# Hybrid diffusion step on one core: weights times values two key tiles at a time, the maxima's row in F32R, neighbourhood tiles of six whole key blocks

## The chip, the cores and the metric

The kernel runs on one core of a Trainium2 chip. A time is the device time of one execution in microseconds (us). TensorE (PE, with its weight loads as PEld), VectorE (DVE), ScalarE (ACT), GpSimd (POOL) and SyncE (SP, which issues DMA) each work through a queue of their own, in order; semaphores join them.

## The reference

Two layers of a transformer trunk work on 1024 latent tokens and 128 prompt tokens of width 1024. A layer has modulated RMS norms, one input projection, three parallel head groups (a convolution module, grouped-query attention with 6 query and 2 key heads of 64, and neighbourhood attention with 6 heads), an output projection, and a squared-ReLU MLP. The two attentions of the latent tokens are what matters here:

```python
# grouped-query: 1024 latent keys and 128 cached context keys
p = softmax(einsum('bqhgd,bkhd->bhgqk', q, k) * Dh ** -0.5)
o = einsum('bhgqk,bkhd->bqhgd', p, v)
# neighbourhood: a latent row of the 16 x 64 grid sees 8 grid rows x 16 columns, and the context
s_loc = where(col_mask, einsum(qr, kr) * scale + bias, NEG_INF)
s_ctx = einsum(qr, kc) * scale
p = softmax(concatenate([s_loc, s_ctx], axis=-1))
o = einsum(p_loc, vr) + einsum(p_ctx, vc)
```

The prompt tokens attend to the prompt alone.

## The kernel before

Everything is F32. Scores and projections split an operand into an F32R part and its rest, and run as F32R products; weights times values, transposes and the row of the maxima are plain F32, which PE does in two passes per product (the page counts both). The order of each engine's instructions is the order in which the program writes them; generators (`prep`, `prompt`, `end`, `natten`, `conv_out`) are advanced by hand so that their pieces lie between those of the main loop. Every PSUM tile is one of eight banks (`P`); SBUF tiles come from the pools S (18), T (18), U (19) and V (24), reused as earlier tiles are read out.

**Grouped-query attention** (`gqa`, L1001) has six units a layer: three pairs of heads, each with two halves of 512 queries. A unit goes over nine key tiles of 128 (eight latent, one of context). A step `kt` makes, for both heads, scores with keys in the partitions (psst, L1132 and L1133; the 65th row of q2 carries the negative maximum of each query), their exponentials on ACT into `pt`, one `side()`, then `late()` of the step before, then another `side()`. `late` is `pv`: weights times values into the accumulator psacc (L1118: two heads in the two halves of PE's columns, so four instructions a key tile), and the sum of `pt` into R (L1120; POOL up to kt 6, DVE after).

`side()` advances the preparation of the next unit (`prep`, L1013): transposes of its queries; twelve calls that each issue two products psm (128 queries by 384 keys, L1044) and their maxima on DVE (mx, L1046); `down` (L1027), which reduces the three maxima of each query to nmx (L1029); `spread` (L1032), which turns nmx into a row by four products with the identity (psnm, L1035), copied by ACT into partition 64 of q2 (L1036). `down(0)` and `spread(0)` come inside the scan, `down(1)` and `spread(1)` behind it, at kt 7. `side()` also advances the prompt's attention and the end of the unit before (pssum, rr, rt). The rest of the convolution (cacc, lsq, lrs, lsg) is spread over the same time on DVE and ACT.

**Neighbourhood attention** (`natten`, L1152) goes over tiles of 128 queries (two grid rows) for two heads at a time. In step `i` it makes the scores of tile i (`scores_na`, L892), its exponentials, the end of tile i-3, transposes of tile i-1 (pspt, L969) with their copies out of PSUM (L977), and weights times values of tile i-2 (pspv, L985), with pieces of the next pair's preparation between. Edge tiles (t below 2 or above 5) see 8 grid rows and the context, 640 keys. Inner tiles see 9 rows and the context, 704 keys: four blocks of 128, the context's 128, and a last block of 64:

```python
self.blocks = [(128 * i, 128, v(r0 // 2 + i)) for i in range(4)]
self.blocks += [(512, 128, vc)] if edge else [(576, 128, vc), (512, 64, v(t + 2, 64))]
```

POOL adds the column mask to the biases of the next pair (L1166 to L1168, `end_bias`), spreads the reciprocal sums (r, L955), and makes the low part of the result (L99, HA<-cc).

Of the kernel before, what the change touches and what calls it, by code (L numbers as in the profile page):

```python
# [45 lines left out]
def hybrid_step(ctx, tc, I, O, depth=DEPTH):  # L46
# [1 line left out]
    pers = ctx.enter_context(tc.tile_pool(name="pers", bufs=1))  # L48
    dram = ctx.enter_context(tc.tile_pool(name="dram", bufs=1, space=bass.MemoryType.DRAM))
    psum = ctx.enter_context(tc.tile_pool(name="psum", bufs=1, space=bass.MemoryType.PSUM))  # L50
    N_S, N_T, N_U = 18, 18, 19

    count = [0]
    def nm(p):
# [9 lines left out]
    def U(shape, dt=F32, n="u"):  # L64
        return pers.tile([128] + list(shape), dt, tag="U", bufs=N_U, name=nm(n))

    def V(shape, n="v"):
        return pers.tile([128] + list(shape), F32, tag="V", bufs=24, name=nm(n))

    def h_views():  # L70

# [34 lines left out]
        nc.vector.tensor_scalar(out=out, in0=a, scalar1=s1, scalar2=s2, op0=op0, **k)  # L106

    ident = pers.tile([128, 128], F32, name="ident")
    ones = pers.tile([128, 128], F32, name="ones")
    eps = pers.tile([128, 1], F32, name="eps")  # L110
    colmask = pers.tile([128, 64], F32, name="colmask")
# [231 lines left out]
    def prologue(pr):  # L343
        nc.scalar.preload_act_table_set("natural_log_exp_and_others")
        make_identity(nc, ident)
        nc.vector.memset(ones, 1.0)
        nc.vector.memset(eps, EPS)
        cc = U([KT, 2], n="cc")
        xt = [S([1024], n="xt") for _ in range(4)]
        for i in range(4):  # L350
            load(xt[i], I["x_sample"][i * 128:(i + 1) * 128, :])
        load(cc, I["cc"])
        load(vecs[0], I["vecs"][0])
        xh = [HF[8 + i][:, 0:1024] for i in range(4)]
        for i in range(4):
            load(xh[i], I["x_sample"][(i + 4) * 128:(i + 5) * 128, :])
        xp = [T([512], n="xtp") for _ in range(2)]
        for b in range(2):
            load(xp[b], I["x_prompt"][:, b * 512:(b + 1) * 512])
        m0 = modulation(0, [0], True)  # L360
        next(m0)
        sg = U([KT, 2], n="sg")
        sigmoid_of(sg, cc)
        tt(silc, cc, sg, ALU.mult)
        norms = [Norm(si) for si in range(3)]
        for k in range(KT):
            X[k] = S([2, HT], n="X")
        run(x_in(0, lambda i, k: xt[i][:, k * 128:(k + 1) * 128], norms[0]))
        del xt
        run(x_in(1, lambda i, k: xh[i][:, k * 128:(k + 1) * 128], norms[1]))  # L370
        next(m0)
        pr.fetch()
        pr.fetch()
        run(x_in(2, lambda i, k: xp[k // 4][:, k % 4 * 128:(k % 4 + 1) * 128], norms[2]))
        del xp
        for _ in range(4):
            next(m0)
        gs = [nrm.rstd() for nrm in norms]
        for _ in range(2):
            for g in gs:  # L380
                next(g)
        run(gs[0])
        for _ in range(2):
            next(m0)
        pr.prep(nc.gpsimd)
        for _ in range(2):
            pr.fetch()
        load(colmask, I["colmask"])
        for l in range(1, depth):
            load(vecs[l], I["vecs"][l])  # L390
        spill(0, 0)
        spill(0, 1)
        run(m0)
        first = norm1(pr.L, 0, norms[0], True)
        next(first)
        pr.prep()
        run(first)
        for g in gs[1:]:
            run(g)
        pr.prep()  # L400
        yield
        yield from together(norm1(pr.L, 2, norms[2], True), norm1(pr.L, 1, norms[1], True))
# [466 lines left out]
    class Direct:  # L869
# [9 lines left out]
        def scores_prompt(self, qs):  # L879
            ps = P("pssp")  # L880
            self.p, self.nmx = [], []
            for j in range(2):
                self.score(ps[:, j * 128:(j + 1) * 128], qs[j], self.kb[j].kp)
            for j in range(2):
                mx = V([1], "mx")
                nc.vector.tensor_reduce(out=mx, in_=ps[:, j * 128:(j + 1) * 128], op=ALU.max, axis=AX.X, negate=True)
                self.p.append(U([128], n="pp"))
                self.nmx.append(mx)
            self.blocks = [(0, 128, [b.vp for b in self.kb])]
            self.src = [ps[:, j * 128:(j + 1) * 128] for j in range(2)]  # L890

        def scores_na(self, qs, t, bias):  # L892
# [2 lines left out]
            nr = 6 if edge else 7  # L895
            o = (t % 4) * 128
            na = nr * 64
            n = na + 256
            if t in (2, 6):
                for x in bias:  # L900
                    limit(x, t == 2)
# [7 lines left out]
            for j in range(2):  # L909
                q = [x[:, o:o + 128] for x in qs[j]]  # L910
                k1, bf = self.kb[j].k1, bias[j]
                p = S([n], n="p")
                pa = P("psa")
                b = pb[:, j * 256:(j + 1) * 256]
                d0 = r0 - 2 * t + 6
                k0 = (r0 + nr) * 64
                z = (d0 + nr) * 64
                main = [(pa[:, 0:na], q, k1[:, r0 * 64:k0])]
                rest = [(b, q, pair(k1[:, k0:k0 + 128], NS - k0, 128))]
                bb = pair(bf[:, z:z + 128], 14 * 64 - z, 128)  # L920
                parts = [(p[:, 0:na], pa[:, 0:na], bf[:, d0 * 64:d0 * 64 + na]),
                         (p[:, na:n].rearrange("p (a b) -> p a b", a=2), b.rearrange("p (a b) -> p a b", a=2), bb)]
                todo += main + rest if j == 0 else rest + main
                jobs.append(parts if j == 0 else parts[::-1])
                self.p.append(p)
# [7 lines left out]
                nc.vector.tensor_reduce(out=nmx, in_=mx, op=ALU.max, axis=AX.X, negate=True)  # L933
                self.nmx.append(nmx)

            def v(i, k=128):
                return [b.v[0:k, i, :] for b in self.kb]

            vc = [x.vc for x in self.kb]
            self.blocks = [(128 * i, 128, v(r0 // 2 + i)) for i in range(4)]  # L940
            self.blocks += [(512, 128, vc)] if edge else [(576, 128, vc), (512, 64, v(t + 2, 64))]
            self.src = self.p

        def exps(self):
# [5 lines left out]
        def transposes(self):  # L950
# [9 lines left out]
            for g, jobs in enumerate(groups):  # L960
                ps = P("pspt")
                pt = (T if nb > 1 else U)([len(jobs) * 128] if nb > 1 else [128], n="pt") if nb > 1 else None
                if pt is None:
                    pts = [U([128], n="pt") for _ in jobs]
                runs = []
                for x, (j, i) in enumerate(jobs):
                    o, n, _ = self.blocks[i]
                    c = slice(x * 128, (x + 1) * 128)
                    nc.tensor.transpose(ps[0:n, c], self.p[j][:, o:o + n], ident)  # L969
                    self.at[j, i] = pt[0:n, c] if pt is not None else pts[x]  # L970
                    if runs and runs[-1][1] == n and pt is not None:
                        runs[-1][2] = x + 1
                    else:
                        runs.append([x, n, x + 1])
                for a, n, b in runs:
                    c = slice(a * 128, b * 128)
                    (nc.vector.tensor_copy if g == 0 and nb > 1 else nc.scalar.copy)(pt[0:n, c] if pt is not None else pts[a], ps[0:n, c])  # L977
            self.p = None

        def pv(self):  # L980
            ps = P("pspv")
            nb = len(self.blocks)
            for i, (_, _, v) in enumerate(self.blocks):
                for j in range(2):
                    mm(ps[64 * j:64 * j + 64, 0:128], v[j], self.at[j, i], start=(i == 0), stop=(i == nb - 1))  # L985
            nc.tensor.transpose(ps[:, 128:256], self.r, ident)
            self.rb = U([128], n="rb")
            acopy(self.rb, ps[:, 128:256])
            self.ps = ps
            self.at = None  # L990
# [10 lines left out]
    def gqa(L):  # L1001
# [11 lines left out]
        def prep(u):  # L1013
# [11 lines left out]
            nmx = []  # L1025

            def down(j):  # L1027
                n = V([4], "nmx")
                nc.vector.tensor_reduce(out=n, in_=mx[j], op=ALU.max, axis=AX.X, negate=True)  # L1029
                nmx.append(n)  # L1030

            def spread(j):  # L1032
                ps = P("psnm")
                for qt in range(4):
                    mm(ps[64:65, qt * 128:(qt + 1) * 128], nmx[j][:, qt:qt + 1], ident, start=True, stop=True)  # L1035
                acopy(qs[u][j][1][64:65, :], ps[64:65, :])  # L1036

            todo = [(j, qt, b) for j in range(2) for qt in range(4) for b in range(3)]
            n = 0
# [62 lines left out]
            yield from k_build(b, True)  # L1102
        yield from prep(0)
        yield
        ending, late = iter(()), None
        for u, (p, si) in enumerate(units):
            L.unit = u
            nxt = prep(u + 1) if u + 1 < len(units) else iter(())
# [3 lines left out]
            pts = {}  # L1112
            kbs = [kb[(2 * p + j) // 3] for j in range(2)]

            def pv(kt, acc, pt, kbs, R, pts):
                for j in range(2):
                    v = kbs[j].v[:, kt, :] if kt < 8 else kbs[j].vc
                    mm(acc[64 * j:64 * j + 64, :], v, pt[:, j, :], start=(kt == 0), stop=(kt == 8))  # L1118
                if kt:
                    tt(R, pts[0] if kt == 1 else R, pt, ALU.add, nc.gpsimd if kt <= GPOOL else nc.vector)  # L1120

# [5 lines left out]
            for kt in range(9):  # L1127
# [7 lines left out]
                pts[kt] = pt  # L1135
                side()
                yield
                if late:
                    late()
                late = partial(pv, kt, acc, pt, kbs, R, pts)  # L1140
                side()
                yield
            run(nxt)
# [1 line left out]
            run(ending)  # L1145
            ending = end(u, acc, R)
            del qs[u]
        late()
        L.pend = ending


# [821 lines left out]
```

## Time and profile before

| what | us |
|---|---|
| time, median of 3 runs (lowest, highest) | 3017.64 (3017.33, 3021.18) |
| the profiled execution: time | 3022.51 |
| its span, first to last instruction | 3020.7 |
| PE busy, share of the span | 2857.6, 95% |
| DVE busy | 2085.0, 69% |
| ACT busy | 1403.4, 46% |
| POOL busy | 650.5, 22% |
| grouped-query attention of the two layers | 351 to 545, 1845 to 2038 |
| neighbourhood attention of the two layers | 545 to 655, 2038 to 2148 |

A row of the timeline has the start, the length of the stretch that it covers, engine, line, operation, output and input by the program's names, the partitions by elements, and how many instructions were merged; a bracket at its end has the idle time before it and what ended that. Matmuls overlap: the cost of one is read from start to next start. psacc<-pt,v and psacc<-pt,vc are weights times values with latent and context values; psnm is the row of the maxima; psm the products for them.

### The profile page before, as it was taken

Reading aid. Unit: us, or ns where it says so; the run is one execution under the profiler, and the core shown is the slowest. Engines: PE = TensorE matmul, PEld = TensorE weight load, DVE = VectorE, ACT = ScalarE, POOL = GpSimd, SP = SyncE. Lnnn points to the kernel's source line nnn. Section 1 sums busy time; section 2 is a strip of 40 time slices with the busy share of each in tenths; the row PEclk is TensorE's granted clock in tenths of the full one; section 3 lists DMA queues with packets and bytes.
Section 4 is the critical chain, followed back from the end, with each engine's and each line's share of the span. In section 5 each row is a group of like instructions: output and inputs, shape, how many; then the busy total and the mean of one; then the engine's idle time right before and its main releaser. Section 6 shows DMA issues by size and latency. Waiting matters only on the chain.

```text
span 3020.7 us, 52765 instructions
## 1 busy us (share of the span) xinstructions
PE 2857.6 (95%) x20328; PEld 2540.2 (84%) x20328; DVE 2085.0 (69%) x3985; ACT 1403.4 (46%) x2880; POOL 650.5 (22%) x607
## 2 busy tenths in 40 slices
PE   6998999999889999999889999999997999999999
PEld 3878745799789999999878886458997999999999
DVE  6587778864767556758665877778557775585676
ACT  4334356763644444433452343568435444434344
POOL 3576345410000000000225762463100000000000
PEclk7999999999999999999989999999998999999999
DMA  7276302423466658443433671024334654575334
GB/s 282 82 209 172 97 24 55 101 81 114 134 197 200 207 165 297 162 154 95 139 122 98 186 205 59 16 59 105 95 119 155 194 174 158 174 253 175 126 96 164
DMA packets 424124, 430.42 MB, mean 142 GB/s; under 512 B 120000, under 2 KB 299968, under 8 KB 423872
## 3 DMA queue, kind: packets, MB, share of 16 engines
q1 hardware_dynamic: 423872, 427.04, 45.4%
q8 instruction: 160, 2.62, 0.4%
q14 instruction: 92, 0.75, 0.1%
HBM read 298.50 MB, written 128.45 MB: 141 GB/s over the span
## 4 chain that ended last, share of the span: by engine, by line
PE 74%; DVE 14%; ACT 4%; DMA 2%; issue 2%; POOL 2%; SPq 1%; DVEq 0%; POOLq 0%; ACTq 0%
PE ps L1319 23%; PE psa L1319 8%; PE psc L1319 7%; PE pso L1319 5%; PE psb L1319 5%; PE psacc L1118 3%; PE pspv L985 2%; DVE cacc L102 2%; PE psd L1319 2%; PE pspt L969 2%; PE psst L1132 2%; PE psm L1044 2%; PE pst L541 1%; PE pst L542 1%; PE pst L543 1%
## 5 line engine op out<-in xcount | busy, mean ns | idle before, releaser
L1319 PE MATMUL ps<-ts,w2h 128*128 128x288 f32 x3072 | 534.4, 296 | 8.3 <-DVE ts L99 4.8
L1319 PEld LDWEIGHTS ps<-ts,w2h 128*128 128x128 f32 x3072 | 451.7, 189 | 9.2 <-DVE ts L99 5.3
L1319 PE MATMUL ps<-ts,w2l 128*128 128x288 f32 x1536 | 329.2, 295 | 0.1
L96 ACT CAST ts<-ti 128x576 fp32r<-128x576 f32 x256 | 172.1, 672 | 314.4 <-PE ps L1319 216.4
L541 PE MATMUL pst<-wh,HA 128*128 128x256 f32 x1040 | 298.8, 287 | 0.0
L542 PE MATMUL pst<-wl,HA 128*128 128x256 f32 x1040 | 295.8, 284 | 0.0
L543 PE MATMUL pst<-wh,HA 128*128 128x256 f32 x1040 | 294.7, 283 | 0.0
L93 ACT ACTIVATE ev<-ev 128x576 f32<-128x576 f32 x224 | 153.7, 686 | 275.0 <-DVE ev L99 271.4
L1319 PEld LDWEIGHTS ps<-ts,w2l 128*128 128x128 f32 x1536 | 247.4, 189 | 0.4 <-DVE w2l L99 0.3
L99 DVE TENSOR_TENSOR ts<-ti,ts 128x576 fp32r<-128x576 f32 x256 | 194.6, 760 | 48.4 <-ACT ts L96 47.6
L102 DVE SCALAR_TENSOR_TENSOR X<-ps,mod,X 128x288 f32<-128x288 f32 x336 | 112.1, 408 | 161.4 <-PE ps L1319 161.4
L541 PEld LDWEIGHTS pst<-wh,HA 128*128 128x128 f32 x1040 | 199.6, 192 | 19.8 <-issue 7.6
L542 PEld LDWEIGHTS pst<-wl,HA 128*128 128x128 f32 x1040 | 199.3, 192 | 0.1
L543 PEld LDWEIGHTS pst<-wh,HA 128*128 128x128 f32 x1040 | 199.3, 192 | 0.0
L99 POOL TENSOR_TENSOR nacc<-nacc,nsq 128x512 f32<-128x512 f32 (+1 forms) x12 | 15.9, 1322 | 836.4 <-PE ps L1319 810.4
L1762 POOL COPY yu<-X 128x128 f32<-128x128 f32 x8 | 3.9, 499 | 855.2 <-DVE X L102 843.2
L99 DVE TENSOR_TENSOR w1l<-w1r,w1h 128x512 fp32r<-128x512 f32 x128 | 87.7, 689 | 133.6 <-ACT w1h L96 130.2
L1319 PE MATMUL pso<-HA,woh 128*128 128x288 f32 x1024 | 177.6, 295 | 0.0
L1046 DVE TENSOR_REDUCE mx<-psm 128x1 f32<-128x384 f32 x288 | 142.2, 546 | 31.9 <-PE psm L1044 31.7
L93 ACT ACTIVATE pt<-psst 128x512 f32<-128x512 f32 x216 | 118.2, 597 | 90.9 <-PE psst L1133 89.9
L99 POOL TENSOR_TENSOR R<-R,pt 128x1024 f32<-128x1024 f32 x60 | 148.3, 2472 | 27.9 <-ACT pt L93 25.9
L1319 PEld LDWEIGHTS pso<-HA,woh 128*128 128x128 f32 x1024 | 149.6, 188 | 0.0
(279 smaller groups left out, 7290.2 us busy)
## 6 DMA issues: line engine op xcount, KB each, us to landing
ti<-hd SPq DMA_DIRECT2D x128, 576.0 KB, 4.0
hd<-ev SPq DMA_DIRECT2D x224, 288.0 KB, 3.8
aw<-in_ada_w SPq DMA_DIRECT2D x160, 256.0 KB, 3.8
w1r<-in_mlp_w SPq DMA_DIRECT2D x160, 256.0 KB, 4.4
HF<-in_mlp_w SPq DMA_DIRECT2D x128, 256.0 KB, 5.1
ddA<-o SPq DMA_DIRECT2D x144, 128.0 KB, 2.9
wr<-in_w_in SPq DMA_DIRECT2D x28, 512.0 KB, 4.0
qd<-ddA SPq DMA_DIRECT2D x48, 256.0 KB, 3.3
```

Source lines behind the costliest of these rows:

```text
L93: nc.scalar.activation(out=out, in_=in_, func=func, scale=scale, bias=bias, **k)
L96: nc.scalar.copy(out, in_)
L99: (eng or nc.vector).tensor_tensor(out=out, in0=a, in1=b, op=op)
L102: nc.vector.scalar_tensor_tensor(out=out, in0=a, scalar=s, in1=b, op0=op0, op1=op1)
L541: mm(o, hi, wh, start=(k == 0), stop=False)
L542: mm(o, hi, wl, start=False, stop=False)
L543: mm(o, lo, wh, start=False, stop=(k == KT - 1))
L969: nc.tensor.transpose(ps[0:n, c], self.p[j][:, o:o + n], ident)
L985: mm(ps[64 * j:64 * j + 64, 0:128], v[j], self.at[j, i], start=(i == 0), stop=(i == nb - 1))
L1046: nc.vector.tensor_reduce(out=mx[j][:, qt, b:b + 1], in_=ps[:, 0:384], op=ALU.max, axis=AX.X)
L1118: mm(acc[64 * j:64 * j + 64, :], v, pt[:, j, :], start=(kt == 0), stop=(kt == 8))
L1319: mm(ps[h][:, 0:HH], x, y[:, h * HH:(h + 1) * HH], start=(start and z == 0), stop=(stop and z == 2), skip_group_check=True)
```

## The change

Three edits, and what they need.

In `gqa`, `late` becomes a list of `pv` pieces that is emptied when two are in it, or at kt 0; the sum into R is a piece of its own (`total`, called through `adding`) and stays one step behind the exponentials.

In `prep`, `down` reduces through a broadcast view, so that each maximum is written twice, in F32R; `spread` multiplies by an F32R identity (`identr`, new, copied from `ident` in the prologue) into partitions 0 and 1, and ACT copies partition 0. The pool U has 18 buffers for 19.

In `scores_na`, an inner tile's scores have 768 columns: 576 of latent keys, a gap of 64 that POOL fills with -1e30, 128 of context. The blocks are six of 128; the fifth takes the whole block `v(t + 2)`, half of it under the gap. The exponentials run over 768, and the last two blocks leave PSUM in one copy of 128x512 on ACT, where there were one of 128x256 and one of 64x256.

```diff
-    N_S, N_T, N_U = 18, 18, 19
+    N_S, N_T, N_U = 18, 18, 18
...
+    identr = pers.tile([128, 128], F32R, name="identr")
...
         make_identity(nc, ident)
+        acopy(identr, ident)
...
-            n = na + 256
+            gap = 0 if edge else 64
+            n = na + 256 + gap
...
                 p = S([n], n="p")
+                if gap:
+                    nc.gpsimd.memset(p[:, 576:640], NEG)
...
-                         (p[:, na:n].rearrange("p (a b) -> p a b", a=2), b.rearrange("p (a b) -> p a b", a=2), bb)]
+                         (pair(p[:, na:na + 128], 128 + gap, 128), b.rearrange("p (a b) -> p a b", a=2), bb)]
...
-            self.blocks = [(128 * i, 128, v(r0 // 2 + i)) for i in range(4)]
-            self.blocks += [(512, 128, vc)] if edge else [(576, 128, vc), (512, 64, v(t + 2, 64))]
+            self.blocks = [(128 * i, v(r0 // 2 + i)) for i in range(4)]
+            self.blocks += [(512, vc)] if edge else [(512, v(t + 2)), (640, vc)]
...
-                    nc.tensor.transpose(ps[0:n, c], self.p[j][:, o:o + n], ident)
...
+                    nc.tensor.transpose(ps[:, c], self.p[j][:, o:o + 128], ident)
...
+                if pt is not None:
+                    (nc.vector.tensor_copy if g == 0 else nc.scalar.copy)(pt, ps[:, 0:len(jobs) * 128])
...
-                n = V([4], "nmx")
-                nc.vector.tensor_reduce(out=n, in_=mx[j], op=ALU.max, axis=AX.X, negate=True)
+                n = V([4, 2], "nmx", F32R)
+                nc.vector.tensor_reduce(out=n, in_=mx[j].unsqueeze(2).to_broadcast([128, 4, 2, 3]), op=ALU.max, axis=AX.X, negate=True)
...
-                    mm(ps[64:65, qt * 128:(qt + 1) * 128], nmx[j][:, qt:qt + 1], ident, start=True, stop=True)
-                acopy(qs[u][j][1][64:65, :], ps[64:65, :])
+                    mm(ps[0:2, qt * 128:(qt + 1) * 128], nmx[j][:, qt, :], identr, start=True, stop=True)
+                acopy(qs[u][j][1][64:65, :], ps[0:1, :])
...
-            def pv(kt, acc, pt, kbs, R, pts):
+            def pv(kt, acc, pt, kbs):
                 for j in range(2):
                     v = kbs[j].v[:, kt, :] if kt < 8 else kbs[j].vc
                     mm(acc[64 * j:64 * j + 64, :], v, pt[:, j, :], start=(kt == 0), stop=(kt == 8))
+
+            def total(kt, pt, R, pts):
                 if kt:
                     tt(R, pts[0] if kt == 1 else R, pt, ALU.add, nc.gpsimd if kt <= GPOOL else nc.vector)
...
-                if late:
-                    late()
-                late = partial(pv, kt, acc, pt, kbs, R, pts)
+                if len(late) == 2 or kt == 0:
+                    while late:
+                        late.pop(0)()
+                if adding:
+                    adding()
+                late.append(partial(pv, kt, acc, pt, kbs))
+                adding = partial(total, kt, pt, R, pts)
                 side()
                 yield
...
-        late()
+        adding()
+        for x in late:
+            x()
```

PE in the second unit of layer 0, around kt 2, before:

```order
L1118 MATMUL psacc_3973<-pt_4013,v_2950 64x512 x2
L1044 MATMUL psm_4100<-k_3045,q_3997 128x384
L1044 MATMUL psm_4103<-k_3045,q_3997 128x384
L1132 MATMUL psst_4107<-q_3737,k_3045 128x512
L1133 MATMUL psst_4107<-q_3746,k_3047 128x512
L1132 MATMUL psst_4111<-q_3744,k_3045 128x512
L1133 MATMUL psst_4111<-q_3759,k_3047 128x512
L1044 MATMUL psm_4116<-k_3045,q_3997 128x384
L1044 MATMUL psm_4119<-k_3045,q_3997 128x384
L1118 MATMUL psacc_3973<-pt_4062,v_2950 64x512 x2
```

The same place now (the numbers of tiles and lines have shifted by a few):

```order
L1119 MATMUL psacc_3975<-pt_3977,v_2952 64x512 x2
L1119 MATMUL psacc_3975<-pt_4015,v_2952 64x512 x2
L1045 MATMUL psm_4102<-k_3047,q_3999 128x384
L1045 MATMUL psm_4105<-k_3047,q_3999 128x384
L1135 MATMUL psst_4109<-q_3739,k_3047 128x512
L1136 MATMUL psst_4109<-q_3748,k_3049 128x512
L1135 MATMUL psst_4113<-q_3746,k_3047 128x512
L1136 MATMUL psst_4113<-q_3761,k_3049 128x512
L1045 MATMUL psm_4118<-k_3047,q_3999 128x384
L1045 MATMUL psm_4121<-k_3047,q_3999 128x384
```

Key tiles 0 and 1 stand together behind the scores of kt 2, and nothing of psacc stands at kt 3; so it goes on with 2 and 3, 4 and 5, 6 and 7, and the ninth tile stands alone behind the next unit's first scores.

PE at the end of the same unit, where `spread(1)` stands, before:

```order
L1133 MATMUL psst_4248<-q_3759,k_3047 128x512
L1118 MATMUL psacc_3973<-pt_4216,v_2950 64x512 x2
L1035 MATMUL psnm_4263<-ident,nmx_4252 1x128 x4
L1132 MATMUL psst_4270<-q_3737,k_3045 128x512
L1133 MATMUL psst_4270<-q_3746,k_3047 128x512
L1132 MATMUL psst_4274<-q_3744,k_3045 128x512
L1133 MATMUL psst_4274<-q_3759,k_3047 128x512
L1118 MATMUL psacc_3973<-pt_4243,v_2950 64x512 x2
```

And now:

```order
L1136 MATMUL psst_4250<-q_3761,k_3049 128x512
L1036 MATMUL psnm_4263<-identr,nmx_4254 2x128 x4
L1135 MATMUL psst_4270<-q_3739,k_3047 128x512
L1136 MATMUL psst_4270<-q_3748,k_3049 128x512
L1135 MATMUL psst_4274<-q_3746,k_3047 128x512
L1136 MATMUL psst_4274<-q_3761,k_3049 128x512
L1119 MATMUL psacc_3975<-pt_4216,v_2952 64x512 x2
L1119 MATMUL psacc_3975<-pt_4245,v_2952 64x512 x2
```

The key tile that stood between the scores of kt 7 and the row of the maxima now stands behind the scores of kt 8.

POOL in the first pair of the neighbourhood attention of layer 0, tiles 3 to 5, now (before, the same rows without the fills of p):

```order
L917 MEMSET p_5584 128x64
L917 MEMSET p_5587 128x64
L99 TENSOR_TENSOR HA_74<-cc_5611,HA_70 128x128
L1175 TENSOR_TENSOR bias_5573<-bias_5573,colmask 128x896
L1176 MEMSET bias_5573 128x128
L1177 COPY bias_5573<-bias_5573 64x64
L960 COPY r_5628<-rs_5626 128x128
L917 MEMSET p_5673 128x64
L917 MEMSET p_5676 128x64
L99 TENSOR_TENSOR HA_74<-cc_5700,HA_70 128x128
```

The fills of tile 4 (p_5673 and p_5676) stand behind the mask added to a bias of the next pair and behind the r of an earlier tile.

More of the change, by code (lines that the diff above doesn't have):

```diff
@@ L65, in U, with V @@
         return pers.tile([128] + list(shape), dt, tag="U", bufs=N_U, name=nm(n))
-    def V(shape, n="v"):
-        return pers.tile([128] + list(shape), F32, tag="V", bufs=24, name=nm(n))
+    def V(shape, n="v", dt=F32):
+        return pers.tile([128] + list(shape), dt, tag="V", bufs=24, name=nm(n))
     def h_views():
@@ L888, in scores_prompt @@
                 self.nmx.append(mx)
-            self.blocks = [(0, 128, [b.vp for b in self.kb])]
+            self.blocks = [(0, [b.vp for b in self.kb])]
             self.src = [ps[:, j * 128:(j + 1) * 128] for j in range(2)]
@@ L934, in scores_na, with v @@
                 self.nmx.append(nmx)
-            def v(i, k=128):
-                return [b.v[0:k, i, :] for b in self.kb]
+            def v(i):
+                return [b.v[:, i, :] for b in self.kb]
             vc = [x.vc for x in self.kb]
-            self.blocks = [(128 * i, 128, v(r0 // 2 + i)) for i in range(4)]
-            self.blocks += [(512, 128, vc)] if edge else [(576, 128, vc), (512, 64, v(t + 2, 64))]
+            self.blocks = [(128 * i, v(r0 // 2 + i)) for i in range(4)]
+            self.blocks += [(512, vc)] if edge else [(512, v(t + 2)), (640, vc)]
             self.src = self.p
@@ L964, in transposes @@
                     pts = [U([128], n="pt") for _ in jobs]
-                runs = []
                 for x, (j, i) in enumerate(jobs):
-                    o, n, _ = self.blocks[i]
+                    o = self.blocks[i][0]
                     c = slice(x * 128, (x + 1) * 128)
[L969 to L977, printed above, removed]
+                    nc.tensor.transpose(ps[:, c], self.p[j][:, o:o + 128], ident)
+                    self.at[j, i] = pt[:, c] if pt is not None else pts[x]
+                    if pt is None:
+                        acopy(pts[x], ps[:, c])
+                if pt is not None:
+                    (nc.vector.tensor_copy if g == 0 else nc.scalar.copy)(pt, ps[:, 0:len(jobs) * 128])
             self.p = None
@@ L982, in pv @@
             nb = len(self.blocks)
-            for i, (_, _, v) in enumerate(self.blocks):
+            for i, (_, v) in enumerate(self.blocks):
                 for j in range(2):
@@ L1104, in gqa @@
         yield
-        ending, late = iter(()), None
+        ending, late, adding = iter(()), [], None
         for u, (p, si) in enumerate(units):
```

## The prediction

> **What bounds the kernel now.** I read the page's busy shares first, then the four stages in which the change works (a table by stretches: PE, PE's weight loads, DVE, ACT and POOL busy, each with its count, then TensorE's granted clock, DMA share and GB/s), then the chain that ended last inside the two grouped-query stretches.
>
> ```profile
> PE 2857.6 (95%) x20328; PEld 2540.2 (84%) x20328; DVE 2085.0 (69%) x3985; ACT 1403.4 (46%) x2880; POOL 650.5 (22%) x607
> ...
> 351.00:545.00 194.00, 180.85 (x807) 95.53 (x806) 151.62 (x258) 112.54 (x236) 104.43 (x56) 0.97 0.12 33
> 545.00:655.00 110.00, 109.82 (x1085) 94.53 (x1084) 88.90 (x346) 88.99 (x254) 31.55 (x83) 1.00 0.39 103
> 1845.00:2038.00 193.00, 181.27 (x800) 95.20 (x799) 149.65 (x254) 112.42 (x236) 105.50 (x56) 0.97 0.12 32
> 2038.00:2148.00 110.00, 109.81 (x1085) 94.52 (x1085) 89.94 (x348) 88.09 (x249) 31.09 (x81) 1.00 0.40 105
> ...
> by line: PE psacc L1118 20.7%; PE psst L1132 12.3%; PE psst L1133 10.6%; PE psm L1044 9.4%; DVE mx L1046 7.1%; PE pstr L784 5.1%; PE psnm L1035 4.2%; DVE cacc L102 4.0%; DVE cacc L99 3.5%; DVE lsq L102 2.9%; PE pssum L1084 2.6%; DVE lrs L10
> ...
> by line: PE psacc L1118 20.0%; PE psst L1132 13.3%; PE psst L1133 11.3%; PE psm L1044 10.2%; DVE mx L1046 6.1%; PE psnm L1035 4.9%; PE pstr L784 4.4%; DVE cacc L99 3.5%; DVE lsq L102 3.0%; PE pssum L1084 2.6%; DVE cacc L102 1.9%; DVE lrs L1
> ```
>
> In the neighbourhood stretches PE stands still for 0.2 us of 110: time taken from PE there is time taken from the kernel. In the grouped-query stretches PE is busy for 93%, DVE for 78%, and the chain changes sides: weights times values (psacc) and the maxima's row (psnm) hold 25% of it, DVE's maxima and the convolution (cacc, lsq, lrs) most of what is not PE. So a microsecond saved on PE counts there only where the chain runs over PE.
>
> **Part 1, two key tiles' weights times values in a row.** The next rows are PE in the third unit of layer 0, then the first modulation, where four column groups of TensorE work without a break, then the two groups of psacc and its weight loads.
>
> ```profile
> 448.42 0.40 PE L1133 MATMUL psst<-q,k 65*128 65x512 f32 x1
> 448.65 0.51 PE L1044 MATMUL psm<-k,q 128*128 128x384 f32 x2
> 449.10 1.08 PE L1118 MATMUL psacc<-pt,v 128*64 128x512 f32 x4
> 450.11 0.62 PE L1044 MATMUL psm<-k,q 128*128 128x384 f32 x2
> 450.56 0.40 PE L1132 MATMUL psst<-q,k 128*128 128x512 f32 x1
> ...
> 40.91 3.62 PE L224 MATMUL psmod<-HF,silc 128*2 128x512 f32 x32
> ...
> L1118 PE MATMUL psacc<-pt,v 128*64 128x512 f32 x384 | 106.6, 634 | 0.0
> L1118 PE MATMUL psacc<-pt,vc 128*64 128x512 f32 x48 | 12.9, 618 | 0.0
> ...
> L1118 PEld LDWEIGHTS psacc<-pt,v x384: 132/136/232, 356.5 to 2036.3; 128*64 128x64 f32 x192
> ```
>
> One key tile is four instructions (two heads side by side in TensorE's columns, two passes of F32): 432 instructions are 108 tiles, nine in each of 12 units. From start to next start a tile takes 450.11 - 449.10 = 1.01 us. Its neighbours pay as well: the pair of psm behind it takes 450.56 - 450.11 = 0.45, the pair ahead of it 449.10 - 448.65 = 0.45, while two passes of 384 columns at the rate of 512 columns in 0.23 (448.42 to 448.65) need about 0.35. So a tile that stands alone costs 1.01 + 0.10 + 0.10 = 1.21. What a second tile behind it costs no row of psacc shows; the nearest is psmod: 32 instructions are 8 passes of the same 512 columns, and with 0.62 for the last one's length (618 ns, the mean in the psacc<-pt,vc row) it is (3.62 - 0.62) / 7 = 0.43 a pass, so 0.87 for a tile. A pair saves 1.21 - 0.87 = 0.34. Tiles 0 to 7 of each unit form four pairs, the ninth stays alone: 48 pairs, 16.3 us gross. On the chain stand 20.7% of 194 and 20.0% of 193, 78.8 us, of the 108 x 1.01 = 109 that all tiles take: 72%. That leaves 11.8 us.
>
> The Trainium skill, "TensorE: Matmul & The Clock Gate", section "Packing small matmuls — row/col tiling", says that a weight load overlaps matmuls in flight only when its row group differs; values use all rows, so by it the second tile's loads would lie bare. The psmod row disagrees here (its groups use all 128 rows too, at 0.43 a pass).
>
> The sums into R stay where they were, a step behind their exponentials; only the PE part is held back, and a weights tile lives one step longer. The wait that it brings: none on exponentials, which are at least as old as before.
>
> **Part 2, the maxima's row.**
>
> ```profile
> 451.64 0.17 DVE L1029 TENSOR_REDUCE nmx<-mx 128x4 f32<-128x12 f32 x1
> ...
> 452.61 1.03 PE L1035 MATMUL psnm<-ident,nmx 128*1 128x128 f32 x8
> 453.58 0.50 PE L1132 MATMUL psst<-q,k 128*128 128x512 f32 x1
> ...
> 397.44 0.22 PE L876 MATMUL pssp<-kp,q 128*128 128x128 f32 x1
> 397.50 0.28 PE L877 MATMUL pssp<-kp,q 128*128 128x128 f32 x1
> 397.62 0.28 PE L876 MATMUL pssp<-kp,q 128*128 128x128 f32 x1
> ...
> L1035 PE MATMUL psnm<-ident,nmx 128*1 128x128 f32 x192 | 25.9, 280 | 10.2 <-DVE nmx L1029 10.2
> ```
>
> 192 instructions are 24 rows of 8 (two passes each). One takes 453.58 - 452.61 = 0.97: eight passes at 0.11 and 0.1 for the change of shape behind them. In F32R four passes remain. F32R passes over 128 columns are in pssp: 0.06 and 0.12 apart. So four cost 0.24 to 0.48, the row 0.34 to 0.58, and it saves 0.39 to 0.63; I take 0.5, the middle. 24 rows, nine tenths of them on the chain (4.2% of 194 and 4.9% of 193 are 17.6 us; the 20 rows inside these stretches take 19.4): 10.8 us. The reduction over twice the elements (0.17 us each now) and the copy from partition 0 instead of 64 I cost at nothing.
>
> **What the new order gives back.** The second row of a unit stood behind a psacc tile; now it comes right behind the scores, 1.0 us sooner, while DVE's maxima come when they came. Ten rows are of this kind (units 0 to 4, both layers). In the rows above DVE was done at 451.81, 0.80 before PE began; six of the ten show no wait like this one, and there I let PE stand for 0.25, a little more than 1.0 - 0.80. The other four wait already (first and last):
>
> ```profile
> 380.87 1.08 PE L1118 MATMUL psacc<-pt,v 128*64 128x512 f32 x4
> 384.47 1.03 PE L1035 MATMUL psnm<-ident,nmx 128*1 128x128 f32 x8 [2.52 <-DVE nmx L1029]
> 387.05 1.97 PE L1118 MATMUL psacc<-pt,v 128*64 128x512 f32 x4
> ...
> 1977.39 0.81 PE L1035 MATMUL psnm<-ident,nmx 128*1 128x128 f32 x6 [0.31 <-DVE nmx L1029]
> ```
>
> Their tile of 1.0 us was hidden in that wait and now comes after it: 4 x 1.0 + 6 x 0.25 = 5.5 us lost. Queued behind the waiting row on PE are the ninth tile's scores, for which ACT's exponentials wait.
>
> **Part 3, six whole blocks.** PE in an inner neighbourhood tile, layer 0 (weights times values: 16 instructions of four blocks, 4 of context, 4 of the half block with 64 rows):
>
> ```profile
> 604.56 1.09 PE L985 MATMUL pspv<-pt,v 128*64 128x128 f32 x16
> 605.48 0.39 PE L985 MATMUL pspv<-pt,vc 128*64 128x128 f32 x4
> 605.80 0.43 PE L985 MATMUL pspv<-pt,v 64*64 64x128 f32 x4
> 606.16 0.33 PE L986 MATMUL pspv<-ident,r 128*128 128x128 f32 x1
> ...
> 558.18 0.89 ACT L93 ACTIVATE p<-p,nmx 128x704 f32<-128x704 f32 x1 [0.51 <-DVE nmx L933]
> ...
> 558.68 0.29 POOL L955 COPY r<-rs 128x128 f32<-128x128 f32 x1
> 559.31 0.88 ACT L93 ACTIVATE p<-p,nmx 128x704 f32<-128x704 f32 x1 [0.16 <-DVE nmx L933]
> ...
> 564.42 0.84 PE L969 MATMUL pspt<-ident,p 128*128 128x128 f32 x5
> ...
> 627.94 0.15 POOL L864 MEMSET bias<- 64x64 f32 x1
> ```
>
> Four blocks take 605.48 - 604.56 = 0.92, the first with 0.05 for its start: 0.22 a block. The context block takes 0.32, since the shape changes behind it, and the half block 0.36 against 0.32 for a last block of full shape. With whole blocks 0.10 + 0.05 = 0.15 goes; 24 inner tiles give 3.6 us, all on PE. The exponentials grow from 704 to 768 elements (0.89 us, 0.08 more each in proportion), two copies out of PSUM become one; both lie beside PE. New is a wait of the exponentials for POOL's fill of the gap, queued behind what POOL has there. The worst place is above, behind the mask added to the next pair's bias: the first head's exponential started at 558.18, POOL is busy until 558.97, two fills take 0.15 each (as the fill of 64 x 64), so it would start 1.1 later. The second head's ends at 560.19 and PE needs both at 564.42: 4.2 us of cover, 3.1 left. With that cover gone four such tiles (the order of POOL in the section on the change shows one; two a layer) would cost 1.1 each, 4.4 us. One U buffer fewer makes reuse tighter by a part of a step, always behind work of the step before; I cost it at nothing, and at 1 us in each of the six prompt tiles, 6 us, if that is wrong.
>
> **The sum.** Grouped-query: 11.8 + 10.8 - 5.5 = 17.1. What becomes late next is DVE: it is busy for 78% and, with 8.5 us off a layer's 194, for 82%, and its pieces of the chain do not shrink. I take a fifth off: 13.7. With 3.6 that is 17 us. The profiled execution took 3022.5 (span 3020.7): 3005.5 by this. It lies 4.9 above the median of 3017.6, for which the forecast is 3000.6. About 0.2%, 6 us, is what a measurement of this kernel tells from no change.
>
> **The rivals.**
> *Half-clock stretches (slower).* After waits PE runs at half its clock for a while:
>
> ```profile
> 381.95:384.47 2.52, 0.00 (x2) 0.00 (x1) 2.45 (x6) 0.00 (x0) 0.00 (x0) 1.00 0.02 5
> 386.00:389.30 3.30, 3.30 (x8) 0.98 (x7) 1.56 (x3) 2.01 (x4) 0.00 (x0) 0.50 0.41 119
> 1877.60:1884.30 6.70, 6.70 (x18) 3.29 (x16) 3.19 (x4) 3.14 (x6) 0.00 (x0) 0.50 0.25 74
> ```
>
> PE idle for 2.52 is followed by 3.3 us at 0.50 (a psacc tile takes 1.97 there), in layer 1 by 6.7. A stretch of 6.7 costs 3.3 us. One more in each of eight of the ten places where the wait for the row grows costs 27: 3017.6 - 17 + 27 = 3027.6; it decides from six on (20). Against it: six of the ten waits grow to 0.25 only. Chance 0.04; two or three such stretches, 7 to 10 lost (3008 to 3011), 0.08. The Trainium skill, "TensorE: Matmul & The Clock Gate", section "The HAM clock gate", has the clock halve after at least one idle window of about 3.4 us. The trace differs: 2.52 was enough.
>
> *Weight loads of the second tile lie bare*, as the rule weighed in part 1 has it. Then 0.136, the load's median, is added to each pass: a pair saves 0.34 - 0.27 = 0.07, part 1 is 48 x 0.07 x 0.72 = 2.4, the sum (2.4 + 10.8 - 5.5) x 0.8 + 3.6 = 9.8: 3007.8. Chance 0.07.
>
> *DVE bounds all units that scan maxima.* Then the second row comes when DVE is ready, whatever PE saved before, and a pair stands behind it where one tile stood: ten times 0.87 more. What pays is twelve second rows (12 x 0.5 = 6.0), the four pairs of unit 5 in two layers (2.7) and the whole blocks (3.6): 12.3 - 8.7 = 3.6, 3014.0. For it: the wait of 2.52; against it: psacc on the chain for 72%, no wait ahead of the row in six of ten places. Chance 0.10.
>
> *The F32R row does not do what it says*, a pass taking 0.22 and the row as long as before: 10.8 x 0.8 = 8.6 less, 3009.2. pssp speaks against it. Chance 0.05.
>
> **How the numbers follow.** The forecast keeps 0.66. Its own range: all pairs and rows on the chain at their best (16.3 + 24 x 0.63 - 5.5 = 25.9, nothing taken off, + 3.6 = 29.5) is 2988.1; with rows at 0.39, the time given back doubled and a third off, (11.8 + 8.4 - 11) x 0.67 + 3.6 = 9.8, it is 3007.8. The rivals between 3008 and 3014 belong in as far as 3013, and the best end is cut a little: 2990 to 3013. Faster means below 3011.6: 0.66, the bare loads' 0.07, 0.04 of the F32R case and half of the mild clock case make 0.81; slower 0.04; within, the rest, 0.15.
>
> **What would show it.** Right: psacc with eight instructions in a row of about 1.9 us start to start; psnm x4 with 0.35 to 0.6 to the next start; waits for nmx ahead of the second row in all ten places; no 64-row block in pspv, its stretch 0.15 shorter, PE still full in the neighbourhood stretches; each grouped-query stretch 6 to 8 us shorter. Wrong: eight psacc at 2.2 or more, psnm passes above 0.2, granted clock under 0.95 in these stretches, PE waiting for p behind POOL's fill.

## The result, and the profile after

The changed kernel takes 3060.2 us (median of 4 runs, 3059.6 to 3061.3), the kernel before 3019.4 in the same series: ratio 1.0133, 95% interval 1.0116 to 1.0151. It is slower by 40 us (35 to 46), where 17 us less were forecast. No rival on record had that size either.

Busy shares of the changed kernel and its span by stretches, in rows that answer to those of before; then one neighbourhood stretch between marks that are the same in both kernels (the first transposition of latent weights to the last context block), layer 0, before and after.

```profile
PE 2856.0 (93%) x20232; PEld 2554.9 (84%) x20232; DVE 2091.5 (68%) x3985; ACT 1406.0 (46%) x2857; POOL 658.9 (22%) x655
```

```profile
347.80:547.00 199.20, 177.60 (x758) 97.07 (x754) 150.83 (x254) 111.77 (x234) 105.48 (x56) 0.91 0.11 31
547.00:670.90 123.90, 113.91 (x1089) 99.13 (x1090) 92.09 (x351) 91.20 (x246) 34.05 (x108) 0.97 0.35 94
1862.70:2059.00 196.30, 174.68 (x756) 95.88 (x753) 150.89 (x253) 111.63 (x234) 105.64 (x56) 0.92 0.12 31
2059.00:2182.90 123.90, 114.15 (x1092) 99.33 (x1091) 92.21 (x351) 91.30 (x246) 34.12 (x109) 0.97 0.35 94
```

```profile
544.80:659.50 114.70, 114.52 (x1134) 98.73 (x1132) 90.40 (x349) 90.79 (x260) 33.04 (x87) 1.00 0.38 100
```

```profile
548.40:677.00 128.60, 118.61 (x1134) 103.33 (x1132) 91.67 (x351) 91.79 (x248) 35.18 (x111) 0.96 0.33 87
```

The neighbourhood stretches, where nothing but a gain was forecast, are 13.9 us longer each (123.9 against 110.0), the grouped-query ones 5.2 and 3.3: together 36.3 of the 37.5 by which the span grew (3058.2 against 3020.7). PE is no longer full: it stands for 10 us in each neighbourhood stretch, and the clock that it is granted falls to 0.97 there, to 0.91 and 0.92 in the others, from 1.00 and 0.97. In the two grouped-query stretches that makes 68 us at half clock, where there were 22 before.

What PE waits for there is a prompt block, in which nothing of the change was meant to happen. First the changed kernel around one of them, PE and ACT; then the same place before.

```profile
582.71 0.27 PE L973 MATMUL pspt<-ident,pp 128*128 128x128 f32 x1
583.00 0.83 ACT L93 ACTIVATE p<-p,nmx 128x640 f32<-128x640 f32 x1 [0.49 <-DVE nmx L938]
...
584.00 0.83 ACT L93 ACTIVATE p<-p,nmx 128x640 f32<-128x640 f32 x1
...
585.02 0.42 ACT L96 CAST q<-pstr 128x128 fp32r<-128x128 f32 x2
...
585.33 0.27 ACT L96 COPY pt<-pspt 128x128 f32<-128x128 f32 x1
...
585.66 0.33 PE L973 MATMUL pspt<-ident,pp 128*128 128x128 f32 x1 [2.68 <-ACT pt L96]
```

```profile
579.10 0.38 PE L969 MATMUL pspt<-ident,pp 128*128 128x128 f32 x2
...
581.73 0.44 ACT L977 COPY pt<-pspt 128x128 f32<-128x128 f32 x2
```

Before, PE issued both transpositions of the pair and went on; ACT copied both 2.6 us later, and nobody waited. Now PE issues one, and the second waits for ACT's copy of the first, which is queued behind two exponentials and three casts. The lines that do this are in the change; the cut diff of the section on it does not show them:

```diff
                 for x, (j, i) in enumerate(jobs):
...
-                for a, n, b in runs:
-                    c = slice(a * 128, b * 128)
-                    (nc.vector.tensor_copy if g == 0 and nb > 1 else nc.scalar.copy)(pt[0:n, c] if pt is not None else pts[a], ps[0:n, c])
+                    if pt is None:
+                        acopy(pts[x], ps[:, c])
```

The copies stood in a loop of their own, behind the transpositions; those of a prompt block (`pt is None`) stand between them now. Each engine's own order is the same as before, so no listing of the order by engine shows it: only the wait is new. The groups of the 24 prompt transpositions (12 pairs), before and after, with PE's idle time ahead of them at the end:

```profile
L969 PE MATMUL pspt<-ident,pp 128*128 128x128 f32 x24 | 5.3, 291 | 1.1 <-ACT pp L93 1.0
```

```profile
L973 PE MATMUL pspt<-ident,pp 128*128 128x128 f32 x24 | 8.2, 344 | 28.3 <-ACT pt L96 24.6 <-ACT pp L93 3.7
```

24.6 us of waiting for the copy, 8.4 of them in each neighbourhood stretch, and around some of the waits PE's clock halves: 1.6 us after the idle of 582.98 to 585.66, and at the end of one of 3.0 us (663.5 to 666.5); behind the middle one, 2.69 us up to 629.45, it does not:

```profile
587.30:590.70 3.40, 3.40 (x15) 3.30 (x15) 2.13 (x11) 1.19 (x3) 0.00 (x0) 0.50 0.00 0
...
665.80:672.60 6.80, 6.11 (x36) 5.54 (x37) 0.36 (x2) 1.46 (x7) 1.38 (x4) 0.50 0.00 0
```

That is 10.2 us at half clock between the marks (548.4 to 677.0), at most 5.1 lost; with three waits of 2.7 to 3.0 (8.4) it makes some 13 of the 13.9. The Trainium skill, "TensorE: Matmul & The Clock Gate", section "The HAM clock gate", puts the halving after an idle window of about 3.4 us; here 2.68 was enough, as 2.52 was before.

The three parts did on PE what was forecast, or more: a pair of key tiles takes 1.87 from start to next start (forecast 1.9), the row 0.23 (0.34 to 0.58), an inner tile's weights times values 1.46 where it took 1.60 (606.16 less 604.56):

```profile
506.14 0.40 PE L1036 MATMUL psnm<-identr,nmx 128*2 128x128 f32 x4
506.37 0.56 PE L1045 MATMUL psm<-k,q 128*128 128x384 f32 x2
...
508.20 1.94 PE L1119 MATMUL psacc<-pt,v 128*64 128x512 f32 x8
510.07 0.62 PE L1045 MATMUL psm<-k,q 128*128 128x384 f32 x2
...
618.94 1.31 PE L986 MATMUL pspv<-pt,v 128*64 128x128 f32 x20
620.08 0.39 PE L986 MATMUL pspv<-pt,vc 128*64 128x128 f32 x4
620.40 0.33 PE L987 MATMUL pspv<-ident,r 128*128 128x128 f32 x1
```

### The profile page after: what moved, and what is told of

The parts are those of the page before. It is cut to its first block, busy times and chain, and to the rows that moved or that the text cites. A ratio compares the mean times of both kernels' runs of the same rounds, so it can differ in the third digit from the quotient of the medians.

```text
span 3058.2 us, 52636 instructions
## 1 busy us (share of the span) xinstructions
PE 2856.0 (93%) x20232; PEld 2554.9 (84%) x20232; DVE 2091.5 (68%) x3985; ACT 1406.0 (46%) x2857; POOL 658.9 (22%) x655
## 4 chain that ended last, share of the span: by engine, by line
PE 72%; DVE 15%; ACT 5%; DMA 3%; issue 2%; POOL 2%; SPq 1%; DVEq 0%; POOLq 0%; ACTq 0%
PE ps L1328 23%; PE psa L1328 8%; PE psc L1328 6%; PE pso L1328 5%; PE psb L1328 5%; PE psacc L1119 3%; DVE mx L1047 2%; PE pst L543 2%; PE pst L544 2%; PE pst L545 2%; PE psd L1328 2%; DVE cacc L102 2%; PE pspv L986 2%; PE pspt L973 2%; PE pstr L786 1%
```

## Experiments

Theory W is the wait in the prompt blocks (in the texts on the parts by themselves, W stands for the forecast's terms); H and the others are named in the texts on record. Ratios are to the kernel before, run on the same chip; 0.1% is 3.0 us.

**The prompt wait, taken out of the changed kernel and put into the kernel before.**

```diff
-                    if pt is None:
-                        acopy(pts[x], ps[:, c])
+                if pt is None:
+                    for x in range(len(jobs)):
+                        acopy(pts[x], ps[:, x * 128:(x + 1) * 128])
```

> The changed kernel, with both transpositions of a prompt block issued ahead of the two copies out of PSUM, as before the change; all else as changed. Theory W (the copy that now stands between the two transpositions makes PE's second one wait for ACT, 12 times, and the waits bring half-clock stretches): the 12 waits go, each neighbourhood stretch shrinks from 123.9 us to 108 to 110, each grouped-query stretch by 4 to 9 us, the whole from 3060 to 3014 to 3023 us. Theory H (the pairs, the row and the fill of the gap cost the time, by waits and half-clock stretches of their own): within 5 us of 3060.

Measured: 3027.3 us, ratio 1.0016 (1.0007 to 1.0025). 35 of the 40 us are gone, the neighbourhood stretch is 115.6 us at full clock, and no wait for a copy is left ahead of the prompt transpositions:

```profile
536.10:651.70 115.60, 113.90 (x1132) 99.28 (x1132) 91.07 (x351) 90.80 (x248) 35.19 (x111) 1.00 0.36 97
```

```profile
L973 PE MATMUL pspt<-ident,pp 128*128 128x128 f32 x24 | 5.9, 300 | 3.8 <-ACT pp L93 3.7
```

W holds and H falls, though the time ends some 4 us above W's range. The edit the other way round, in the kernel before:

```diff
                     self.at[j, i] = pt[0:n, c] if pt is not None else pts[x]
+                    if pt is None:
+                        acopy(pts[x], ps[:, c])
+                        continue
```

> The kernel before, with one edit alone: each of the two prompt transpositions is followed at once by its copy. Theory W: slower by the 27 us of both neighbourhood stretches and by 8 to 18 us in the grouped-query stretches, 3054 to 3064 us. Theory H: no change, 3016 to 3022 us.

Measured: 3044.4 us, ratio 1.0082 (1.0070 to 1.0095), 25 us slower with nothing else changed, some 10 below W's range. Both neighbourhood stretches are 127.7, 13.0 more than before:

```profile
540.70:668.40 127.70, 119.39 (x1134) 102.62 (x1132) 90.94 (x349) 91.53 (x260) 32.96 (x87) 0.96 0.34 89
```

```profile
L969 PE MATMUL pspt<-ident,pp 128*128 128x128 f32 x24 | 7.8, 326 | 23.2 <-ACT pt L96 22.2 <-ACT pp L93 1.0
```

So the edit alone makes W's 26 us there, and next to nothing in the grouped-query stretches, where W had 8 to 18. With the other parts it costs 35. Of the ten beyond, 2 to 6 lie in unit 5, the last before the neighbourhood: from its first scores to the first mark the changed kernel takes 33.2 and 33.1 us in the two layers, at a clock of 0.90, the two runs without the wait for a copy 30.0 (copies behind, clock 1.00) and 32.2 or 32.1 (two tiles, the run that follows, clock 0.95). Here, in the kernel before, the same wait of 1.97 brought no half clock. The rest was not separated.

**Which of the two it is, the order or the tile.** One more PSUM tile, order untouched:

```diff
                     c = slice(x * 128, (x + 1) * 128)
+                    if pt is None and x:
+                        ps = P("pspt")
```

> The changed kernel, order untouched, but the second prompt transposition writes a PSUM tile of its own instead of the other half of the first one's. Theory W (PE waits because the second transposition writes the tile that ACT's first copy still reads, though other columns of it): as with both transpositions ahead, 3022 to 3030 us, and no wait for a copy ahead of the second transposition. Rival (the order itself costs, ACT's copies stand in the way whatever tile is written): 3055 to 3062 us.

Measured: 3025.2 us, ratio 1.0019 (1.0009 to 1.0028), and no wait for a copy in the group:

```profile
L975 PE MATMUL pspt<-ident,pp 128*128 128x128 f32 x24 | 6.3, 305 | 5.0 <-ACT pp L93 3.7 <-DVE mx L1049 1.3
```

The wait hung on the tile: the second transposition writes other columns than the copy reads, and waited all the same as long as both lay in one tile.

**The parts by themselves.** Part 1 alone (`late`, `total`, `adding` of the diff, in the kernel before):

> The kernel before with part 1 alone: weights times values of two key tiles in a row; the row of maxima stays F32, the neighbourhood tiles stay as they were. Theory W with the terms of the forecast: 11.8 - 5.5 = 6.3, a fifth off, 5 us faster, 3014 us. Theory H: the second rows come 1.0 us sooner, wait, and bring 13.6 us of half-clock loss as seen after the change, 3025 to 3030 us.

Measured: 3033.3 us, ratio 1.0037 (1.0024 to 1.0051), 11 us slower: above H's range too, and far from the forecast's terms. Part 2 alone:

> The kernel before with part 2 alone: the row of maxima in F32R (and one U buffer fewer, which its identity needs). Theory W with the terms of the forecast: 24 rows x 0.5 x 0.9 = 10.8, a fifth off, 8.6 us faster, 3011 us. Theory H: what the row saves is waited for at its next DVE result: 3017 to 3022 us.

Measured: 3012.0 us, ratio 0.9975 (0.9964 to 0.9985), 7.6 us faster: W's 3011, by 1 us. Part 3 alone, filled by GpSimd as in the change, then by VectorE (`nc.vector.memset` for `nc.gpsimd.memset`):

> The kernel before with part 3 alone (six whole blocks, the gap filled by GpSimd), the two prompt transpositions ahead of their copies. Theory F (the exponentials wait for GpSimd's fill behind the mask of the bias, and PE then for the copies queued behind them on ACT): the 3.6 us that the whole blocks save are given back at two places a layer, 1 to 2.5 us each layer, so 3018 to 3022 us, no change. The forecast's own term, waits hidden: 3.6 us faster, 3016 us.

> As the run with the blocks alone, but the gap is filled by VectorE instead of GpSimd. Theory F: the waits for GpSimd go, 2 to 4 us below the run with GpSimd's fill, 3015 to 3018 us. If the fill is hidden either way: the same time as that run, or a little more, since VectorE has 48 more instructions.

Measured: 3022.5 us, ratio 1.0013 (1.0003 to 1.0022), and 3019.7 us, ratio 1.0002 (0.9992 to 1.0012): the first 0.5, the second 1.7 above F's ranges. With GpSimd's fill the exponentials stood behind the mask of the bias, and PE behind the copies that ACT then did late:

```profile
2083.93 2.10 POOL L1166 TENSOR_TENSOR bias<-bias,colmask 128x896 f32<-128x896 f32 x1 [2.06 <-DMA bias<-in_rpb]
...
2086.77 0.23 POOL L915 MEMSET p<- 128x64 f32 x2
...
2086.95 0.94 ACT L93 ACTIVATE p<-p,nmx 128x768 f32<-128x768 f32 x1 [3.52 <-POOL p L915]
...
2089.95 0.66 PE L784 MATMUL pstr<-ident,kd 128*128 128x128 f32 x4 [1.03 <-ACT pt L977]
```

With VectorE's fill no exponential of these tiles waits for GpSimd, and the two neighbourhood stretches are shorter than before (114.7) by 1.1 and 0.7; with GpSimd's they take 114.6 and 116.6:

```profile
545.40:659.00 113.60, 113.26 (x1134) 99.34 (x1132) 92.58 (x373) 91.60 (x248) 33.07 (x87) 1.00 0.38 100
2037.00:2151.00 114.00, 113.41 (x1132) 99.31 (x1132) 92.83 (x375) 91.62 (x248) 33.05 (x87) 1.00 0.38 100
```

F's places are seen, and the traces differ by F's 2 to 4 us (3.6); the 3 us between the two runs' times are at the edge of what their intervals tell apart. Parts and prompt edit add up: 24.8 + 11.2 - 7.6 + 3.9 = 32 of 40.

**Why pairs cost.** Two tests: tiles 6 and 7 left single in units 0 to 4, and the next unit's scores shared out otherwise (`side(n)` takes n pieces of its preparation).

```diff
-                if len(late) == 2 or kt == 0:
+                if len(late) == 2 or kt == 0 or (u < 5 and kt >= 7):
```

> Part 1 alone, but in units 0 to 4 tiles 6 and 7 stay single, so that one tile stands behind the second row, as before the change, and not a pair. Theory D: the 10 x 0.87 = 8.7 us behind the row go, the pairs' saving ahead of it stays worth nothing, unit 5 keeps its 2.7: 3017 to 3022 us. Rival L (the lumps cost: PE waits for VectorE in the steps without values, VectorE idles in the pairs, and three pairs are left): 3027 to 3032 us.

Measured: 3022.3 us, ratio 1.0009 (0.9999 to 1.0019): just above D's range, 8 us below the pairs alone.

```diff
-                side()
+                side(1 + (kt > 1 and kt % 2 == 0))
...
-                side()
+                side(1 - (0 < kt < 8 and kt % 2))
```

> Part 1 alone, as in the run with the pairs only, but the next unit's scores for its maxima are shared out otherwise: none in the step without values, twice as many just ahead of each pair, so that VectorE has maxima to search while PE runs a pair. Rival L (VectorE idles in the pairs and PE waits between them): VectorE's idle time inside the search falls and the whole comes 4 to 8 us below the pairs alone, 3025 to 3029 us. Theory D (VectorE's work up to the last maximum is the same, and a pair still stands behind the second row): within 3 us of the pairs alone, 3030 to 3036 us.

Measured: 3021.4 us, ratio 1.0004 (0.9994 to 1.0014), below both ranges: 10 us under the pairs alone, more than L forecast, where D forecast at most 3. A table worked out from the traces shows where the time lies (layer 1, us): the search, from VectorE's first maximum (mx<-psm) of a unit to the end of its last, plus the tail from there to the next unit's first scores; unit 5 searches nothing and stands with its whole length. Idle is VectorE's inside the five searches.

```
                     u0         u1         u2         u3         u4        searches tails idle  unit 5
before           26.6+5.4   21.8+4.1   24.3+4.1   21.6+3.4   18.1+4.0    112.4    20.9  10.4   29.8
pairs only       28.2+4.2   21.3+4.2   26.3+4.2   21.3+4.2   18.7+4.2    115.8    21.1  13.6   28.3
single tail      28.2+3.4   21.3+4.1   25.1+4.1   21.3+3.4   18.7+4.1    114.6    19.0  12.4   29.9
search moved     29.2+4.5   20.8+3.8   23.6+3.8   21.4+3.1   19.6+3.1    114.6    18.2  14.4   28.3
```

The pairs save PE 0.34 three times in each search, 5 us a layer, and the searches together got no shorter by it: u1 and u3 lost 0.2 to 1.0, u0 and u4 grew, and u2 grew in two of the three. D says as much, but it is not shown: VectorE idles for 10 of the 112 us already before, and D's other forecast failed. L's own sign is missing: with the scores moved VectorE idles more, not less. What fell is the tail, since that edit also put the ninth tile's scores ahead of the second row, so that only the pair stands behind it.

H's half clock, which D leaves out, is in the trace of the pairs alone. The two grouped-query stretches, 193.7 and 193.5 us at 0.97 before:

```profile
345.30:545.20 199.90, 182.34 (x806) 99.62 (x805) 151.11 (x254) 112.27 (x236) 104.88 (x56) 0.93 0.12 33
1846.20:2041.60 195.40, 177.80 (x805) 97.67 (x805) 150.81 (x255) 111.87 (x236) 105.00 (x56) 0.96 0.12 34
```

They hold 43 us at half clock, where before had 22 and the single tail 28; half of the difference, at most, is lost. So the 8 us by which the single tail is better can be D's tails or the clock; the runs do not tell them apart. It also takes the gain of unit 5 where it falls there: 29.9 for the single tail in the table, though its unit 5 has pairs.

The longer searches are 1.6 us in u0 and 2.0 in u2. In u2 PE ran 10.2 us at half clock, before 3.4. There is a wait of 2.9 for a maximum in both, but with pairs the half clock begins at 1929.64, ahead of that wait (1930.92 to 1933.84); why stays open. In u0 it is the convolution; pairs alone, then before:

```profile
1850.76 2.43 POOL L99 TENSOR_TENSOR R<-pt,pt 128x1024 f32<-128x1024 f32 x1 [34.22 <-ACT pt L93]
...
1851.97 5.89 DVE L102 SCALAR_TENSOR_TENSOR cacc<-cin,vecs,cacc 128x1167 f32<-128x1167 f32 x2
...
1853.31 3.31 POOL L99 TENSOR_TENSOR R<-R,pt 128x1024 f32<-128x1024 f32 x1
...
1857.91 2.05 PE L729 MATMUL psmu<-cacc,ones 128*128 128x512 f32 x2 [4.17 <-DVE cacc L102]
```

```profile
1851.04 3.85 DVE L102 SCALAR_TENSOR_TENSOR cacc<-cin,vecs,cacc 128x1167 f32<-128x1167 f32 x2
...
1853.59 3.51 POOL L99 TENSOR_TENSOR R<-R,pt 128x1024 f32<-128x1024 f32 x1 [1.40 <-ACT pt L93]
...
1854.95 1.12 PE L729 MATMUL psmu<-cacc,ones 128*128 128x512 f32 x2 [0.81 <-DVE cacc L102]
```

Without a tile's values ahead of them, the scores of kt 2 and their exponentials come sooner against the convolution, GpSimd's next sum starts at 1853.31 while VectorE is still in its first piece, and the two pieces take 5.89 instead of 3.85. The second piece makes the difference, with pairs, then before:

```profile
1854.46 3.39 DVE L102 SCALAR_TENSOR_TENSOR cacc<-cin,vecs,cacc 128x1167 f32<-128x1167 f32 x1
```

```profile
1853.46 1.43 DVE L102 SCALAR_TENSOR_TENSOR cacc<-cin,vecs,cacc 128x1167 f32<-128x1167 f32 x1
```

With pairs it starts behind the sum and ends 1.2 us after it; before, it started 0.13 ahead of the sum, and the sum took the longer time (3.51). PE waits 4.17 for the pieces, and its clock halves. u0 also varies by itself: 28.2 us in layer 0 before, and 28.2 and 31.0 in the two layers of the run with the row and pairs in unit 5. The Trainium skill, "SBUF — State Buffer", section "SBUF: two separate sides", says that a VectorE operation with two inputs from SBUF and a GpSimd operation that reads SBUF lock each other out for a whole instruction; the trace agrees: whichever of the piece and the sum began second took 3.39 or 3.51.

**Where pairs pay, and the best of both.** Row plus pairs in unit 5 alone; then row and blocks (fill by VectorE, prompt copies behind both transpositions), without pairs and with pairs in unit 5.

```diff
-                if len(late) == 2 or kt == 0:
+                if len(late) == (2 if u == 5 else 1) or kt == 0:
```

> The kernel before with the row of maxima in F32R (part 2) and pairs of key tiles in unit 5 alone, the one unit in which no next unit's maxima are searched. Theory D (VectorE's maxima set when the second row of units 0 to 4 comes; pairs pay only where no maxima are searched): 2 x 1.4 = 2.7 us below the row alone (3012), 3009 us. If pairs cost by themselves, also without maxima: 3012 to 3016 us.

> Parts 2 and 3 without part 1: the row of maxima in F32R, six whole blocks with the gap filled by VectorE, both prompt transpositions ahead of their copies. Sum of the parts as measured alone, -7.6 for the row and 0 for the blocks: 3009 to 3014 us. If the whole blocks pay the 1.8 us a layer once the fill is off GpSimd: 3008 to 3010 us.

> As the run with the row and the blocks, and pairs of key tiles in unit 5 alone, where no maxima are searched. Theory D: 2 x 1.4 = 2.8 us below that run, unit 5 at 28.3 us where it was 29.8; the best of all versions, 3006 to 3010 us. If pairs give nothing there either: the same time as that run.

Measured, in this order: 3012.5 us, ratio 0.9984 (0.9974 to 0.9993); 3010.1 us, 0.9959 (0.9945 to 0.9973); 3010.6 us, 0.9971 (0.9958 to 0.9984). Unit 5 takes 28.4 us in both layers with pairs (first and third), 29.8 without (second): there the 1.4 come. The whole does not show them: by their times the first and the third fall on the side of no gain, but 2.8 us are less than the intervals. Row and blocks without pairs are 12 us (8 to 17) faster than the kernel before, the lowest here, though not told apart from the version with pairs in unit 5 or from the row alone.

## Why the prediction was wrong

- **Part 3, "two copies out of PSUM become one; both lie beside PE".** This is the step that failed, 25 to 35 of the 40 us. It was priced for inner tiles alone. The same loop serves prompt blocks, whose copies the edit puts between the two transpositions; the prediction has no term for them, which is a wait put at nothing without a reason. It meets prompt tiles once, as six users of U buffers; twelve blocks pass through the loop. The trace of before had the price: in a neighbourhood stretch ACT's copies came 2.6 us after the transpositions, and 2.7 to 3.0 is what PE waited there.
- **Part 1, "that leaves 11.8 us".** 72% of the saving was counted because 72% of the tiles' time lay on the chain. The instruction prices were right (1.87 a pair), and in unit 5, where no half clock fell, the pairs paid (1.4 of 1.36 forecast). In the ten units with a search, PE's share of the chain was no room to gain: the searches together got no shorter. The rival "DVE bounds all units that scan maxima" (chance 0.10) comes nearest; its own terms give part 1 alone 2.7 - 8.7 = 6 us slower. Measured alone: +11 for -6.3 x 0.8. Whether VectorE's pace or the half clock makes the cost stays open.
- **The time given back.** The waits came in all ten second rows, as said: together 10.6 us in the changed kernel, 5.6 before, so 5.0 more for the 5.5 forecast. With pairs alone the tail of u3 grew by about the 0.87 of the rival (3.4 to 4.2); those of u1, u2 and u4, where PE had not waited before, by 0.1 to 0.2.
- **Part 2.** Right in its direction, with the term mis-sized: 0.23 a row, so 0.74 saved, not 0.5. Unit 4 shows it: 27.6 to 26.3 us, two rows in the unit. Measured alone it is -7.6 for the 8.6 forecast, but with 0.74 the same sum gives 24 x 0.74 x 0.9 x 0.8 = 12.8: the near hit is luck in part. The trace of that run gives part of the saving back at half clock (0.94 and 0.95 in the grouped-query stretches, 0.97 before).
- **Part 3, the blocks.** 0.15 a tile was right (1.60 to 1.46). The cover for the fill "4.2 us, 3.1 left" was not there at two places a layer: the bound of 4.4 with the cover gone was what the run showed (+3.9, 0.9 to 6.6). With the fill off GpSimd 0.7 to 1.1 of the 1.8 a layer is left.
- **Half-clock stretches, chance 0.04.** They came (0.91 and 0.92 in the grouped-query stretches), but mostly in other places than the second rows that the rival named. Of the 46 us more at half clock there, 17 stand beside prompt copies, 14 beside the convolution, 7 in the search of u2 and 7 beside second rows.

## What to carry to other kernels

An edit to a shared helper must be read for every kind of block that passes through it, and a consumer moved between two producers of one tile makes the second producer wait, even if no engine's order changes and the columns differ: look for the new pair of engines, and take the price from how late the consumer stood before. A share on the chain says where time is spent, not that shortening it moves the end: ask which engine's work sets the next meeting point (here perhaps VectorE's maxima), and do not count savings of another engine ahead of it before a run shows them. A short wait can cost more than its length where half clock follows, so read the granted clock of each stretch beside its waits. Time each part of a change alone; here one small part out of three was worth keeping as it stood.

## What the runs showed of the hardware

- PE's clock halved for 3.4 or 6.8 us beside idle times of 2.68 and 3.00 us in a stretch that had run at full clock, and not behind one of 2.69: the three waits there cost about one and a half times their length (8.4 us of waits, some 13 lost).
- F32R passes over 128 columns with two rows out take 0.06 us each (four in 0.23), the lower end of what the prompt scores had shown.
- GpSimd's sum over 1024 elements and a piece of VectorE's convolution held each other up: begun 0.13 us ahead of the sum the piece took 1.43 us and the sum 3.51; begun 1.15 behind it the piece took 3.39.
- A transposition into one half of a PSUM tile waited for ACT's copy out of the other half, 24.6 us in twelve places; with two tiles and the same order no wait for a copy was left.
